# Splitting eleven weight units of the stick-breaking layer early, and keeping the two parts in DRAM

## The chip, the cores and the metric

The kernel runs on one core of a Trainium2 chip. The metric is the time of one execution on the device in microseconds. The engines of the core are TensorE (PE, with its weight loads PEld), VectorE (DVE), ScalarE (ACT), GpSimd (POOL) and SyncE (SP), which here only issues DMAs.

## The reference, cut to what matters

Two blocks follow each other on 512 tokens of width 1024, all in float32.

The first block is a hybrid layer: a norm, one wide projection `proj = h @ w_in`, a state-space branch with a convolution over four tokens, a sliding-window attention branch, gates, an output projection, and then 64 routed experts.

The second block puts 16 learned tokens in front (528 rows) and runs a stick-breaking attention layer, a wide layer with a squared ReLU, a differential attention layer and another wide layer. What the change touches is the projection of the stick-breaking layer:

```python
hn = rmsnorm(h, a_norm_g[i])
qkv = (hn @ a_w_qkv[i]).reshape(B, T, 3, SB_HEADS, SB_HEAD_DIM)
q, k, v = (qkv[:, :, x].transpose(0, 2, 1, 3) for x in range(3))   # cut
o = stick_breaking_attention(q, k, v)   # weights sigmoid(z) * product of (1 - sigmoid(z)) over later keys
h = h + merge_heads(o) @ a_w_o[i]
```

The matrix `a_w_qkv` is an input: nothing has to be computed before its split can be made.

## The kernel before

**Split matmuls.** A float32 product is computed as three matmuls of a rounded type: each operand is split into a high part (a copy that rounds, on ScalarE) and a low part (operand minus high part, on VectorE), and the products high x high, high x low and low x high are summed (`mm3`, `mm3s`). Every weight matrix is laid out on the host in units of 256 output columns: 128 partitions by 2048 floats, 1 MB. A unit is loaded by SyncE into one of three buffers `raw` (`load`, line 139) and split into one of two buffers `wh` and one of two `wl`.

**The first block's projections.** `block1_body` first normalizes and transposes x. Then `dense_x` (units 0 to 3 of the state-space columns) makes two tiles per unit: 24 matmuls of 512 columns, then the convolution on ScalarE and VectorE, a tanh one tile later, and a store of the result to DRAM. After it come six units of the query, key, value and time-step columns, each with four token tiles of 24 matmuls. Their results stay on the chip in twelve `dq` tiles. The window attention (`swa`) begins after that, with further units of `dense_x` and `dense_z` woven between its steps.

Working tiles of the first block come from one pool of 44 slots of 128 partitions by 516 floats (`S`). Results of matmuls lie in eight banks.

**The stick-breaking layer.** It has 12 units: for each of four groups of heads one unit of q, one of k and one of v. The list is made in `a_units` (line 779), followed by eight pieces of the output weights. `ahead` and `start_unit` (line 170) load a unit, take its two split buffers, and prepare four split pieces of 512 columns; `tick` issues one piece while the unit before it is being multiplied, and `take` issues what is left, hands the unit out and starts the next. The first unit is loaded and split at the end of the experts. `layer_a` runs the units of group 0 at once, and weaves those of groups 1 to 3 between the steps of the heads (`sb_steps`): scores on TensorE, softplus on VectorE and ScalarE, a scan on VectorE (L2029), a subtraction on GpSimd (L2030), an exponential on ScalarE (L2031), then transpositions and the product with v. In this part TensorE's instructions keep the order in which they are written.

**What else sets the order.** Apart from the instructions that are pinned, a list scheduler decides the order on every engine ahead of time, SyncE's queue included: instructions stand in the order in which they would be ready in its own model, earlier program positions first. On the chip every engine then works through its list in order, so a DMA that waits for a semaphore holds up the DMAs behind it.

Of the kernel before, what the change touches and what calls it, by code (L numbers as in the profile page):

```python
# [9 lines left out]
F32 = mybir.dt.float32  # L10
F32R = mybir.dt.float32r
# [55 lines left out]
class K:  # L67
# [47 lines left out]
    def pin(self, ins):  # L115
        return self.tc.keep_in_program_order(ins)
# [53 lines left out]
    def start_unit(self):  # L170
        self.unit = None
        if self.units:
            src, w, K = self.units.pop(0)
            pin, self.pin_unit = self.pin if self.pin_unit else lambda x: x, False
            raw = self.load(src, w)
            h = self.st.tile([128, 2112], F32R, tag="wh", bufs=self.NSPL, name="wh")
            l = self.st.tile([128, 2112], F32R, tag="wl", bufs=self.NSPL, name="wl")

            def pieces():
                for i in range(0, w, w // 4):  # L180
                    x = slice(i, i + w // 4)
                    pin(self.nc.scalar.activation(h[:, x], raw[:, x], AF.Copy))
                    pin(self.nc.vector.tensor_tensor(l[:, x], raw[:, x], h[:, x].bitcast(F32), op=ALU.subtract))  # L183
                    yield
            self.unit = [t[:, :w].rearrange("p (k c) -> p k c", k=K) for t in (h, l)], pieces()
# [113 lines left out]
    def rest(self, fills):  # L299
        for f in fills:  # L300
            for _ in f:
                pass


    def block1(self):
        pool = self.tc.tile_pool
        with pool(name="cp1", bufs=1) as self.cp, pool(name="sm1", bufs=1) as self.sm, pool(name="act1", bufs=1) as self.act:
            self.block1_body()

    def block1_body(self):  # L310
# [12 lines left out]
        conv = self.small(I["conv"], [128, 24, 5], "conv")  # L323
# [15 lines left out]
        with self.in_order("scalar", "vector"):  # L339
            W0 = self.split_steps(raw0, 2048)  # L340
# [6 lines left out]
            W0 = [next(W0), self.load_split(I["w_xbc"][1], 2048)]  # L347
# [12 lines left out]
                            ("gate_d", [2, 512, 1024]), ("oT_d", [8, 128, 512])):  # L360
            setattr(self, name, self.dr.tile(shape, F32, name=name))
        self.wide = 2
        self.rest([self.dense_x(conv, 0, 4, W0)])


        cs = self.sincos(posi)
# [6 lines left out]
        for u in range(6):  # L373
            w = 264 if u < 4 else 256
            src = I["w_dq264"][u] if u < 4 else I["w_dq256"][u - 4]
            wh, wl = self.load_split(src, 8 * w)
            for t in range(4):
                p = self.PD()
                ts = slice(t * 128, (t + 1) * 128)
                self.mm3(p[:, :w], lambda k: hh[k][:, ts], lambda k: hl[k][:, ts], lambda k: wh[:, k], lambda k: wl[:, k])  # L380
                self.evac(dq[t][u // 2][:, (u % 2) * 256:(u % 2 + 1) * 256], p[:, :256])
                if u < 4:
                    nc.vector.tensor_copy(dtr[:, t, 8 * u:8 * u + 8], p[:, 256:264])
            if u == 3:
                self.dt_prep(dtr, dtb, alg)

        self.wide = 1
        fills = [self.dense_x(conv, 4, 12), self.dense_z(0, 4)]
# [35 lines left out]
        for _ in self.ssd_out(3, self.last_norm, acc):  # L424
            n, t = step // 4, step % 4
# [353 lines left out]
    def a_units(self):  # L779

        W = self.I["a_w_o"]
        return [(self.I["a_w_qkv"][i + hg], 2048, 8) for hg in range(4) for i in (0, 4, 8)] + [(W[u][:, :1280], 1280, 5) for u in range(4)] \
            + [(W[u][:, 1280:], 768, 3) for u in range(4)]

    def last_rows(self):
# [1861 lines left out]
```

## Time and profile before

| | us |
|---|---|
| median of 3 runs | 2669.95 (2668.76 to 2676.37) |
| the profiled execution | 2671.22 |
| its span, first to last instruction | 2669.4 |
| TensorE busy in the span | 2534.5 |
| VectorE, ScalarE, GpSimd busy | 1517.1, 1108.8, 538.0 |
| mean granted clock of TensorE | 0.982 |

Busy time is the union of an engine's instructions. In a row of the windows view, each engine has its busy time in that stretch and, in brackets, the number of its instructions; the clock is the granted share of full speed, and the DMA share is the mean over 16 engines. An instruction's row ends with the idle time before it and what ended it. The first block's projections lie from about 22 to 140 us, the experts from about 740 to 1260 us, the stick-breaking layer from about 1290 to 1630 us.

### The profile page before, as it was taken

The page shows a single profiled execution, that of the slowest core. Times are in us where ns is not written, and L with a number is a line of the kernel's source. Part 1 is how long each engine was busy: PE and PEld are TensorE (multiplying, and loading weights), DVE is VectorE, ACT ScalarE, POOL GpSimd, SP SyncE. Part 2 cuts the span into 40 slices and gives each one's busy share as a digit, 9 for nine tenths or more (in the row PEclk, how much of TensorE's full clock was granted, in tenths as well). Part 3 has the DMA queues.
Part 4 walks back from the last instruction along what each step waited for, and adds up shares of the span by engine and source line. Part 5 has one row for each costly group of instructions (what it writes and reads, how often), then busy time and mean ns, then how long its engine had stood idle before and what let it go on. Part 6 is the DMA issues. An engine that isn't in the chain of part 4 may idle for free. (4 is left out here: it accounts for less than half of the span.)

```text
span 2669.4 us, 43757 instructions
## 1 busy us (share of the span) xinstructions
PE 2534.5 (95%) x17386; PEld 2114.4 (79%) x17386; DVE 1517.1 (57%) x3166; ACT 1108.8 (42%) x2261; POOL 538.0 (20%) x537
## 2 busy tenths in 40 slices
PE   7998999999979998997999999999999899999999
PEld 5987769879955555553888889999999777788887
DVE  6488666686652222224588886334467878634433
ACT  5356644433311111112498764223245766523321
POOL 0043532221121100111154420001102445100000
PEclk9999999999989999999899999999999999999999
DMA  5223365445399999998311323222231011322221
GB/s 191 94 103 131 115 202 179 165 146 187 111 388 392 419 419 419 411 384 344 113 57 37 114 76 118 95 94 82 95 116 64 32 57 49 118 81 94 95 95 63
DMA packets 111360, 436.86 MB, mean 164 GB/s; under 512 B 16441, under 2 KB 37353, under 8 KB 68912
## 3 DMA queue, kind: packets, MB, share of 16 engines
q1 hardware_dynamic: 105488, 429.33, 43.3%
q0 software_dynamic: 5520, 4.63, 0.7%
q8 instruction: 138, 2.26, 0.3%
q14 instruction: 70, 0.57, 0.1%
q10 hardware_dynamic: 144, 0.07, 0.0%
HBM read 400.65 MB, written 43.79 MB: 166 GB/s over the span
## 5 line engine op out<-in xcount | busy, mean ns | idle before, releaser
L210 DVE TENSOR_TENSOR wl<-raw,wh 128x1024 fp32r<-128x1024 f32 (+2 forms) x228 | 280.4, 1260 | 212.5 <-ACT wh L209 208.5
L232 PE MATMUL pd<-hh,wh 128*128 128x512 f32 (+2 forms) x1152 | 393.9, 343 | 4.4 <-DVE zth L1333 2.9
L232 PE MATMUL pd<-hl,wh 128*128 128x512 f32 (+2 forms) x1152 | 392.9, 342 | 2.7 <-DVE hl L213 2.7
L232 PE MATMUL pd<-hh,wl 128*128 128x512 f32 (+2 forms) x1152 | 393.7, 343 | 1.0 <-DVE wl L245 1.0
L209 ACT ACTIVATE wh<-raw 128x1024 fp32r<-128x1024 f32 (+2 forms) x228 | 222.7, 1022 | 412.9 <-PE pd L232 312.7
L232 PE MATMUL pd<-wh,hh 128*128 128x256 f32 (+2 forms) x936 | 266.8, 285 | 4.5 <-DVE vt L2380 1.8
L232 PE MATMUL pd<-wl,hh 128*128 128x256 f32 (+2 forms) x936 | 264.1, 282 | 2.2 <-DVE wl L213 2.2
L232 PE MATMUL pd<-wh,hl 128*128 128x256 f32 (+2 forms) x936 | 264.4, 283 | 0.0
L232 PEld LDWEIGHTS pd<-hh,wh 128*128 128x128 f32 x1152 | 218.3, 190 | 30.1 <-DVE zth L1333 3.1
L232 PEld LDWEIGHTS pd<-hl,wh 128*128 128x128 f32 x1152 | 218.6, 190 | 29.0 <-DVE hl L213 2.9
L232 PEld LDWEIGHTS pd<-hh,wl 128*128 128x128 f32 x1152 | 218.3, 190 | 27.3 <-DVE wl L245 1.9
L1027 PE MATMUL pd<-mraw,xg 128*48 128x256 f32 x2048 | 237.6, 384 | 2.2 <-DMA mraw<-in_w_moe 2.2
L1027 PEld LDWEIGHTS pd<-mraw,xg 128*48 128x48 f32 x2048 | 128.2, 124 | 92.5 <-issue 10.8
L232 PEld LDWEIGHTS pd<-wh,hh 128*128 128x128 f32 (+1 forms) x936 | 170.5, 182 | 10.3 <-issue 2.7
L232 PEld LDWEIGHTS pd<-wl,hh 128*128 128x128 f32 (+1 forms) x936 | 170.4, 182 | 4.4 <-DVE wl L213 2.7
L232 PEld LDWEIGHTS pd<-wh,hl 128*128 128x128 f32 (+1 forms) x936 | 170.1, 182 | 1.9 <-issue 0.2
L1035 DVE TENSOR_TENSOR sg<-lo,pd 48x256 f32<-48x256 f32 x64 | 27.1, 423 | 223.3 <-ACT lo L1034 223.3
L987 POOL DMA_INDIRECT y_d<-ys,idx x64 | 60.5, 945 | 435.0 <-DVE ys L1061 411.1
L232 PE MATMUL pd<-vh,wl 128*128 128x272 f32 (+1 forms) x512 | 145.2, 285 | 0.0
L232 PE MATMUL pd<-vl,wh 128*128 128x272 f32 (+1 forms) x512 | 145.2, 285 | 0.0
L232 PE MATMUL pd<-vh,wh 128*128 128x272 f32 (+1 forms) x512 | 143.5, 284 | 0.0
L232 PE MATMUL pd<-wh,xh 128*128 128x256 f32 (+1 forms) x384 | 124.0, 325 | 0.5 <-DVE acc L1399 0.3
(593 smaller groups left out, 6150.7 us busy)
## 6 DMA issues: line engine op xcount, KB each, us to landing
mraw<-in_w_moe SPq DMA_DIRECT2D x192, 1024.0 KB
raw<-in_mlp_w_in SPq DMA_DIRECT2D x32, 1024.0 KB
raw<-in_mlp_w_out SPq DMA_DIRECT2D x32, 1024.0 KB
raw<-in_w_xbc SPq DMA_DIRECT2D x12, 1024.0 KB
raw<-in_a_w_qkv SPq DMA_DIRECT2D x12, 1024.0 KB
raw<-in_w_z SPq DMA_DIRECT2D x8, 1024.0 KB
raw<-in_w_gate_in SPq DMA_DIRECT2D x8, 1024.0 KB
bc<-acT_d SPq DMA_DIRECT2D x32, 256.0 KB
```

Source lines behind the costliest of these rows:

```text
L209: nc.scalar.activation(h, src, AF.Copy)
L210: nc.vector.tensor_tensor(l, src, h.bitcast(F32), op=ALU.subtract)
L232: self.nc.tensor.matmul(*a, **kw)
L987: x = self.nc.gpsimd.indirect_dma_start(out=self.y_d[:, :], out_offset=bass.IndirectOffsetOnAxis(ap=rows, axis=0), in_=y[0:64 + self.CAP], ...
L1027: self.pin(self.nc.tensor.matmul(p[64 * i:64 * i + self.CAP, 0:256], lhsT=x[:, k], rhs=w[i][:, k], start=k == 0, stop=k == 7))
L1035: self.nc.vector.tensor_tensor(sg[0:CAP], lo, p[64:64 + CAP, 0:256], op=ALU.mult)
```

## The change

Units 1 to 11 of `a_w_qkv` are no longer loaded and split in the layer. A new generator `presplit` walks through them in steps of 512 columns: a load of 256 KB into a working tile, a copy on ScalarE, a subtraction on VectorE, and two stores of 256 KB into a new DRAM tensor `aw_d`, one for the high parts and one for the low parts. There are 44 steps. Two are issued after each of the last six of the first eight convolution tiles; then one or two after each token tile of the six units that follow; what is left, if anything, before the window attention. In the layer `start_unit` loads the two parts of such a unit straight into `wh` and `wl`, on SyncE, when the unit is started, and its `pieces` yield nothing. Unit 0 and the output weights are split as before.

```diff
-            raw = self.load(src, w)
+            raw = None if isinstance(src, list) else self.load(src, w)
             h = self.st.tile([128, 2112], F32R, tag="wh", bufs=self.NSPL, name="wh")
             l = self.st.tile([128, 2112], F32R, tag="wl", bufs=self.NSPL, name="wl")
 
+            if raw is None:
+                for t, x in zip((h, l), src):
+                    self.nc.sync.dma_start(t[:, :w].bitcast(F32), x)
+
             def pieces():
-                for i in range(0, w, w // 4):
+                for i in range(0, w if raw is not None else 0, w // 4):
...
+    def presplit(self):
+
+        self.aw_d = self.dr.tile([2, 12, 128, 2048], F32, name="aw_d")
+        for u in range(1, 12):
+            for c in range(0, 2048, 512):
+                c = slice(c, c + 512)
+                raw, h, l = self.S(name="awr")[:, :512], self.S(F32R, name="awh")[:, :512], self.S(F32R, name="awl")[:, :512]
+                self.nc.sync.dma_start(raw, self.I["a_w_qkv"][u, :, c])
+                self.split_to(h, l, raw)
+                for x, y in enumerate((h, l)):
+                    self.nc.sync.dma_start(self.aw_d[x, u, :, c], y.bitcast(F32))
+                yield 1
...
-        self.rest([self.dense_x(conv, 0, 4, W0)])
+        pre = self.presplit()
+        for i, _ in enumerate(self.dense_x(conv, 0, 4, W0)):
+            for _ in range(2 if i > 1 else 0):
+                next(pre)
...
                 if u < 4:
                     nc.vector.tensor_copy(dtr[:, t, 8 * u:8 * u + 8], p[:, 256:264])
+                for _ in range(1 + (t % 2)):
+                    next(pre, None)
             if u == 3:
                 self.dt_prep(dtr, dtb, alg)
+        self.rest([pre])
...
-        return [(self.I["a_w_qkv"][i + hg], 2048, 8) for hg in range(4) for i in (0, 4, 8)] + [(W[u][:, :1280], 1280, 5) for u in range(4)] \
+        return [((self.I["a_w_qkv"][i + hg] if hg + i == 0 else [self.aw_d[x, i + hg] for x in range(2)]), 2048, 8) for hg in range(4) for i in (0, 4, 8)] + [(W[u][:, :1280], 1280, 5) for u in range(4)] \
```

## Rows read from the trace of the kernel before

**Rows 1.** The page, parts 1 and 2: span, and TensorE's busy time

```profile
span 2669.4 us, 43757 instructions
...
PE 2534.5 (95%) x17386; PEld 2114.4 (79%) x17386; DVE 1517.1 (57%) x3166; ACT 1108.8 (42%) x2261; POOL 538.0 (20%) x537
```

**Rows 2.** Windows view: stretch, length, busy time (count) per engine, clock, DMA, GB/s

```profile
20.00:140.00 120.00, 117.24 (x787) 106.38 (x785) 67.91 (x141) 56.45 (x83) 3.41 (x3) 1.00 0.32 112
140.00:170.00 30.00, 30.00 (x133) 24.16 (x132) 22.64 (x36) 17.53 (x26) 11.54 (x14) 1.00 0.38 132
170.00:200.00 30.00, 30.00 (x131) 24.02 (x130) 27.98 (x51) 16.07 (x25) 16.32 (x24) 1.00 0.27 95
200.00:220.00 20.00, 13.98 (x60) 10.77 (x58) 19.83 (x33) 13.49 (x20) 9.56 (x12) 0.91 0.50 172
1340.00:1520.00 180.00, 162.66 (x1230) 152.19 (x1229) 149.77 (x282) 148.76 (x309) 85.98 (x73) 0.94 0.22 70
...
1290.00:1340.00 50.00, 46.77 (x362) 44.33 (x361) 29.32 (x55) 25.23 (x49) 11.30 (x11) 0.93 0.20 68
```

**Rows 3.** Waits of TensorE, 1340 to 1520 us: total, times, longest

```profile
PE pm L245 <- ACT zs L2031: 8.8, 4, 3.4
PE pd L245 <- DVE kT L1885: 3.4, 2, 1.9
...
PE pd L245 <- DVE wl L183: 2.3, 3, 0.8
PE pd L245 <- ACT wh L182: 0.5, 1, 0.5
```

**Rows 4.** Timeline in the layer: start, duration, engine, line, operation, idle before

```profile
1375.79 2.19 ACT L182 ACTIVATE wh<-raw 128x512 fp32r<-128x512 f32 x4
...
1400.52 2.21 ACT L182 ACTIVATE wh<-raw 128x512 fp32r<-128x512 f32 x4
...
1402.90 1.89 DVE L183 TENSOR_TENSOR wl<-raw,wh 128x512 fp32r<-128x512 f32 x3
...
1403.98 0.63 ACT L2031 ACTIVATE zs<-zs 128x528 f32<-128x528 f32 x1
...
1404.66 1.33 PE L245 MATMUL pm<-consts,zs 128*128 128x128 f32 x5 [3.41 <-ACT zs L2031]
```

**Rows 5.** Windows view in steps of 2 us around that wait

```profile
1400.00:1402.00 2.00, 0.55 (x3) 0.31 (x3) 2.00 (x5) 2.00 (x5) 1.30 (x1) 1.00 0.30 70
...
1404.00:1406.00 2.00, 1.34 (x6) 1.26 (x7) 2.00 (x5) 2.00 (x5) 0.15 (x1) 0.50 0.45 61
```

**Rows 6.** Groups by form, 1290 to 1520 us: count, busy us, mean ns

```profile
L183 DVE TENSOR_TENSOR wl<-raw,wh 128x512 fp32r<-128x512 f32 x44 | 34.5, 830 | 1.4 <-ACT wh L182 1.3
...
L183 DVE TENSOR_TENSOR wl<-raw,wh 128x320 fp32r<-128x320 f32 x4 | 1.7, 478 | 0.0
...
L182 ACT ACTIVATE wh<-raw 128x512 fp32r<-128x512 f32 x44 | 24.2, 621 | 9.1 <-PE pd L232 9.1
L182 ACT ACTIVATE wh<-raw 128x320 fp32r<-128x320 f32 x4 | 1.5, 454 | 0.0
```

**Rows 7.** Windows view of the split's two lines alone, VectorE's and ScalarE's

```profile
1340.00:1520.00 180.00, 25.23 (x32) 0.94 0.22 70
...
1340.00:1520.00 180.00, 16.82 (x32) 0.94 0.22 70
```

**Rows 8.** The split's subtraction over the whole run: shortest, median, longest ns

```profile
L183 DVE TENSOR_TENSOR wl<-raw,wh x80: 342/678/1814, 1255.4 to 1600.0; 128x512 fp32r<-128x512 f32 x48, 128x320 fp32r<-128x320 f32 x16, 128x192 fp32r<-128x192 f32 x16
```

**Rows 9.** Windows view of two stretches in which DMA is crowded

```profile
1490.00:1500.00 10.00, 9.53 (x79) 9.30 (x77) 9.55 (x16) 7.78 (x16) 3.60 (x4) 1.00 1.01 366
...
425.00:430.00 5.00, 4.37 (x40) 3.98 (x39) 5.00 (x6) 3.58 (x6) 3.17 (x2) 1.00 0.99 341
```

**Rows 10.** Timeline of SyncE in the first block's projections

```profile
61.74 0.33 SPq L142 DMA_DIRECT2D raw<-in_w_dq  x1
...
72.95 0.33 SPq L142 DMA_DIRECT2D raw<-in_w_dq  x1
```

**Rows 11.** Waits of TensorE, 20 to 250 us

```profile
PE pm L1294 <- DVE cr L1481: 4.1, 1, 4.1
```

## The prediction

> **What bounds the kernel now.** I read the page first, then the windows view over the two stretches that the change touches, then the waits of TensorE, the timeline behind its longest wait, and last the rows of the split itself. The page says that TensorE is busy for 2534.5 of 2669.4 us, so only 135 us of the whole span are idle, and an edit can win time only where such idle time lies [rows 1]. The windows view shows where it does not lie: from 20 to 140 us, the first block's projections, TensorE is busy for 117.2 of 120 us at full clock, and from 140 to 200 us without a gap; VectorE and ScalarE are little more than half busy before 140 us [rows 2]. From 1340 to 1520 us, the heads of the stick-breaking layer, the picture is another: TensorE is busy for 162.7 of 180 us, VectorE for 149.8, ScalarE for 148.8, and the granted clock is 0.94. With levels of 2.4 and 1.2 GHz that mean says that some 0.12 x 180 = 21.6 us ran at the lower one.
>
> The waits there name ScalarE's exponential (zs L2031) for 8.8 us in 4 waits, then VectorE's kT for 3.4, and the split's own wl and wh for 2.8 us [rows 3]. The timeline behind one 3.41 us wait shows why: ScalarE starts four split pieces at 1400.52 and the exponential, for which TensorE stands, starts at 1403.98; VectorE has three of the subtractions from 1402.90 on [rows 4]. Behind that gap the clock is at its lower level: 1.00 from 1400 to 1402 us, 0.50 from 1404 to 1406 us [rows 5]. TensorE's order is written out there, so it stops whenever the chain score, softmax, exponential, transposition is late by more than the projections put in between can fill. So the limit of this stretch is that chain on two engines that are 83% busy, and the split is load that need not be on them.
>
> **What the change takes out of the layer.** Eleven units of four pieces leave: 44 VectorE subtractions, 34.5 us busy, and 44 ScalarE copies, 24.2 us [rows 6]. Sixteen pairs run from 1290 to 1340 us, where VectorE and ScalarE are little more than half busy and TensorE 46.8 of 50 us [rows 2]; I cost those at nothing, and if all that idle time were theirs they would be worth 3 us. The other 28 pairs, seven units, lie between 1340 and 1520 us. The split takes 25.2 us of VectorE and 16.8 us of ScalarE there, of which four smaller pieces of the output weights (1.7 and 1.5 us) stay [rows 6, 7]. So VectorE falls from 149.8 to 126.3 us and ScalarE from 148.8 to 133.5 us: 70% and 74% of the stretch instead of 83%. What can be won is the idle time, 180 - 162.7 = 17.3 us, and the work not done at the lower clock, 21.6 / 2 = 10.8 us, if every such dip follows a gap as the one shown does: 28 us in all. The least is nothing: of the waits only 2.8 us name the split itself, and the scans and the work on GpSimd in the chain stay. Seven bursts, each of which holds ScalarE for 2.2 us, set the chain back by 15 us if none of it is covered, which with the clock comes near the upper end. I take half of the 28 us, 14 us; both ends stay in the range.
>
> The split's VectorE pieces take 830 ns on average in this stretch, while their median over the run is 678 ns and the longest is 1814 ns [rows 6, 8], so they also suffer from something beside them. The Trainium skill (SBUF — State Buffer, section Who interferes with whom) says that a VectorE instruction with two inputs in SBUF and a GpSimd instruction that reads SBUF exclude each other for a whole instruction, and the split has two such inputs. By that rule the GpSimd steps of the chain would also get shorter, and the saving would lie nearer to 20 us than 14; the rows show only that the pieces are stretched, not what they do to GpSimd.
>
> **What it adds in the layer.** Instead of one load of 1 MB per unit there are two, straight into the buffers that TensorE reads. 11 MB more over some 230 us, where DMA is busy for 22% [rows 2], is nothing. But the buffers are two deep: a unit's load can start only when TensorE has finished with the unit before the last, and its wait stands in SyncE's queue ahead of whatever follows (stores of head outputs, later loads). Two megabytes at the 366 GB/s of the nearest crowded stretch [rows 9] take 5.7 us; two consecutive bursts lie 25 us apart [rows 4], so some 19 us of cover are left and I cost it at nothing. If that cover went, each unit would cost up to 6 us. The first such unit needs a buffer that the combination of the expert outputs reads last, and is wanted only after the 96 matmuls of unit 0, which come behind that combination.
>
> **What it adds in the first block.** 44 steps, 12 beside the convolution tiles and the rest beside the next projection. Each has a load of 256 KB, one copy, one subtraction, and two stores of 256 KB. On VectorE that is 44 x 0.68 = 30 us, on ScalarE 44 x 0.62 = 27 us (the same shape in [rows 6, 8]). From 20 to 140 us VectorE is idle for 52 and ScalarE for 64 us [rows 2], so both fit, and TensorE has eight banks of results to run ahead of late evacuations. On SyncE 132 issues of 0.33 us [rows 10] make 44 us, which fits too.
>
> DMA is tighter. The steps move 132 x 256 KB = 34.6 MB. The trace moves transfers of this size at 341 GB/s where the engines are 99% busy [rows 9]; that makes 101 us. The engines are 32% busy over the 120 us, so 82 us are free [rows 2]. Some 19 us of transfers, a fifth of the steps, are therefore left at 140 us. Eight or nine steps, 6 us of VectorE, then fall in the stretch from 140 to 220 us, where VectorE is busy for 70.5 of 80 us and where TensorE already stops 4.1 us for VectorE's cr [rows 2, 11]. What could hide it is the 7 us that VectorE has free until 170 us. I take 5 us of loss. The lower end is 0; the upper is that TensorE itself follows DMA, 19 us, and more where the queue's order is bad: I allow 30.
>
> The Trainium skill (DMA: Bandwidth & Descriptors, section Rules for kernel authors) asks for 1 MiB or more per transfer, and its section on the anatomy of one DMA gives, for DMAs issued by GpSimd, a fit of 2.0 us and the bytes at 436 GB/s; by it 256 KB take an estimated 2.6 us, 343 us for all if none overlapped. The row of 341 GB/s at transfers of this size speaks against the serial reading: there they overlap.
>
> **The sum.** The profiled execution took 2671.2 us: 2669.4 of span and 1.8 around it. 2671.2 - 14 + 5 = 2662.2. The median of the three timed runs is 2669.95, 1.3 us below that execution, so the forecast is 2661 us, faster by 0.34%. I treat 0.3%, 8 us, as what a measurement here can tell from nothing. Its own range, gain 8 to 20 us and loss 0 to 8, is 2648 to 2668.
>
> **Rivals.**
> 1. *The gain is not there* (26%). The chain of scans, GpSimd subtraction and exponential sets the pace, and the pieces only filled its gaps. For it: the waits on the split itself are 2.8 us of 17.3 idle, and the 3.4 us for kT name a projection's result, which no piece makes. Against: both engines are 83% busy, and the longest wait has pieces right before it [rows 3, 4]. Gain 4, loss 4: 2670 us.
> 2. *DMA holds the first block* (23%, slower). SyncE's queue is one order fixed ahead of time. If the stores of a step stand in it before a projection's weights and the loads land later than planned, the weights wait, and ScalarE and VectorE stand at a piece whose data is missing, ahead of the weight split. A projection unit takes 11.2 us between its loads [rows 10]; six steps beside it bring 4.7 MB, with its own weights 5.8 MB, 17 us at 341 GB/s. That is 6 us too much per unit, over six units 36 us, of which loads up to three units ahead and the idle DMA time at the start cover a sixth to a half. It decides once the transfers in front of a weight load exceed what three buffered units cover, some 25 us. Price 19 to 30 us: 2661 + 24 = 2685.
> 3. *The new loads stand in SyncE's queue at the wrong place in the layer* (4%, slower): a wait for TensorE's release ahead of the stores that free score buffers. Seven units at 3 us with the gain lost: 2690 us.
>
> The remaining 47% is the forecast. Faster by over 0.3%: 0.47; within 0.3%: 0.26; slower by over 0.3%: 0.27. For 8 times in 10 the range takes in rival 1 and most of rival 2: 2642 to 2689 us, the low end being most of the 28 us won at no cost.
>
> **What the profile after would show.** Right: in the layer VectorE's and ScalarE's busy time down by 24 and 15 us, waits for zs and wl gone or halved, the stretch shorter by some 14 us and its clock above 0.94; from 20 to 140 us DMA busy above 80% with TensorE still at 117 of 120 us; VectorE a few us busier from 140 to 220 us. Wrong: TensorE waiting for wh or wl of the projections between 60 and 170 us (rival 2), waits for zs of the same length in the layer (rival 1), or TensorE waiting for a DMA into wh or wl there (rival 3).

## The result, and the profile after

The changed kernel takes 2808.11 us (median of five runs, 2801.80 to 2812.21) where the kernel before takes 2673.17 us: a ratio of 1.0502, 95% interval 1.0490 to 1.0515. Forecast were 2661 us and a range of 2642 to 2689. It is 135 us slower, and the range missed it by 119 us.

The page of the changed kernel, to be set beside [rows 1]: TensorE executes the same number of matmuls, yet it is idle for 2800.0 - 2547.7 = 252 us instead of 135.

```profile
span 2800.0 us, 44077 instructions
...
PE 2547.7 (91%) x17386; PEld 2126.0 (76%) x17386; DVE 1514.7 (54%) x3166; ACT 1111.4 (40%) x2261; POOL 539.7 (19%) x537
```

Three instructions that both kernels have serve as milestones: the load of `iota`, issued when the experts begin; the first `lastq`, ahead of the stick-breaking layer; and the last sum of squares (`pm<-sq,ones`), behind its heads. Each row gives an instruction's count, its min/median/max in ns, and the starts of the first and the last one. First the kernel before, then the changed one:

```profile
L659 SPq DMA_DIRECT2D iota<-in_consts x1: 333/333/333, 738.1 to 738.1; - x1
...
L126 DVE TENSOR_SCALAR lastq<-iota,slot,gw x8: 406/408/414, 1228.3 to 1231.9; 128x256 f32<-128x256 f32 x8
...
L1705 PE MATMUL pm<-sq,ones x8: 377/386/392, 1305.8 to 1629.2; 128*128 128x256 f32 x4, 128*128 128x272 f32 x4
```

```profile
L682 SPq DMA_DIRECT2D iota<-in_consts x1: 333/333/333, 884.4 to 884.4; - x1
...
L126 DVE TENSOR_SCALAR lastq<-iota,slot,gw x8: 403/409/412, 1374.7 to 1378.3; 128x256 f32<-128x256 f32 x8
...
L1728 PE MATMUL pm<-sq,ones x8: 377/386/393, 1450.5 to 1762.1; 128*128 128x256 f32 x4, 128*128 128x272 f32 x4
```

Up to the experts 884.4 - 738.1 = 146.3 us are lost. The stick-breaking layer, from `lastq` to the last sum of squares, is 387.4 us long instead of 400.9: 13.5 us won. The difference of the two is 132.8 us. The two traces differ by 2800.0 - 2669.4 = 130.6 us; the 2 us between these numbers lie behind the layer. So the layer gains about as much as was forecast, and the whole miss lies in the first block.

The windows view of the changed kernel, with the columns of [rows 2]. The last row is the stretch that answers to 1340 to 1520 us of before, 144.7 us later:

```profile
20.00:140.00 120.00, 92.83 (x526) 81.77 (x525) 62.59 (x115) 48.33 (x72) 0.20 (x2) 0.89 0.63 196
140.00:170.00 30.00, 7.81 (x65) 7.59 (x63) 8.42 (x12) 6.94 (x9) 0.00 (x0) 0.71 0.74 218
170.00:200.00 30.00, 8.56 (x48) 8.38 (x48) 6.50 (x19) 4.32 (x8) 0.00 (x0) 0.61 0.55 160
...
40.00:290.00 250.00, 142.28 (x820) 128.59 (x820) 87.53 (x174) 75.70 (x120) 8.02 (x7) 0.77 0.63 194
1484.70:1664.70 180.00, 169.26 (x1344) 158.99 (x1343) 142.91 (x273) 147.09 (x308) 92.46 (x83) 0.98 0.38 130
```

The kernel before does the same 820 matmuls from 40 us on in about half that time:

```profile
40.00:166.00 126.00, 125.23 (x821) 113.91 (x820) 72.91 (x155) 56.09 (x86) 13.47 (x16) 1.00 0.33 115
```

From 40 to 290 us TensorE stands still for 107.7 us, and its 820 matmuls take 142.3 us instead of 125.2, at a mean granted clock of 0.77 instead of 1.00. That is 124 of the 146 us. The other 22 us are lost behind it: from there to the `iota` load the changed kernel takes 884.4 - 290 = 594.4 us, the kernel before 738.1 - 166 = 572.1 us. And from 140 to 200 us no engine is near its limit: VectorE and ScalarE work for 28% of the time or less, and DMA is 74% and 55% busy. Where every resource has room, the time must go into waiting, so the next view is the waits. First TensorE from 20 to 420 us, then ScalarE and SyncE's queue up to 350 us (total, times, longest, in us):

```profile
PE pd L236 <- DVE dtr L403: 50.2, 3, 39.7
PE pd L236 <- ACT cc L1496: 32.4, 6, 13.8
PE pd L236 <- DVE acT L1150: 18.9, 1, 18.9
...
ACT awh L213 <- DMA awr<-in_a_w_qkv: 164.4, 42, 6.6
...
SPq L318 <- ACT awh L213: 142.5, 38, 5.5
```

TensorE waits for banks that copies of its results have to empty (`dtr` on VectorE, `cc` on ScalarE). ScalarE waits for the load of a step, 42 times for 44 steps; and SyncE's queue waits for ScalarE's copy of a step, 38 times. These two wait for each other in turn, as the timeline of two steps shows (start, duration, engine, line; the idle time before it in brackets):

```profile
154.54 0.63 ACT L213 ACTIVATE awh<-awr 128x512 fp32r<-128x512 f32 x1 [5.41 <-DMA awr<-in_a_w_qkv]
...
155.19 0.32 SPq L318 DMA_DIRECT2D aw_d<-awh  x1
155.20 0.69 DVE L214 TENSOR_TENSOR awl<-awr,awh 128x512 fp32r<-128x512 f32 x1 [5.35 <-ACT awh L213]
155.56 0.42 SPq L315 DMA_DIRECT2D awr<-in_a_w_qkv  x1
156.08 0.40 SPq L318 DMA_DIRECT2D aw_d<-awl  x1
...
159.72 0.63 ACT L213 ACTIVATE awh<-awr 128x512 fp32r<-128x512 f32 x1 [2.66 <-DMA awr<-in_a_w_qkv]
160.38 0.32 SPq L318 DMA_DIRECT2D aw_d<-awh  x1
160.38 0.69 DVE L214 TENSOR_TENSOR awl<-awr,awh 128x512 fp32r<-128x512 f32 x1 [1.88 <-ACT awh L213]
160.75 0.42 SPq L315 DMA_DIRECT2D awr<-in_a_w_qkv  x1
```

Read it in a circle. The copy ends at 155.17; only then can SyncE issue the store of the high part (155.19), which stands in its queue ahead of the next load (155.56); that load lands just before the next copy (159.72); and so on. One load of a step is on its way at a time. The rows of the two tiles give the length of a round: the load lands 4.1 us (median) after its issue, the copy takes 0.63, the store's and the load's issue 0.3 to 0.4 each, and 43 rounds lie between the first copy and the last, (281.5 - 48.7) / 43 = 5.41 us each:

```profile
L315 SPq DMA_DIRECT2D awr<-in_a_w_qkv x44: 336/424/832, 41.9 to 278.1; - x44
...
DMA to landing us min/median/max: 3.1/4.1/6.3
...
L213 ACT ACTIVATE awh<-awr x44: 615/630/636, 48.7 to 281.5; 128x512 fp32r<-128x512 f32 x44
```

What that does to TensorE is seen in VectorE's list while TensorE stands for 39.7 us (VectorE from 148 to 188 us, and TensorE's next matmul; the subtractions at 155.20 and 160.38 are shown above):

```profile
149.16 0.69 DVE L214 TENSOR_TENSOR awl<-awr,awh 128x512 fp32r<-128x512 f32 x1 [1.92 <-ACT awh L213]
...
165.44 0.69 DVE L214 TENSOR_TENSOR awl<-awr,awh 128x512 fp32r<-128x512 f32 x1 [4.36 <-ACT awh L213]
171.73 0.69 DVE L214 TENSOR_TENSOR awl<-awr,awh 128x512 fp32r<-128x512 f32 x1 [5.60 <-ACT awh L213]
176.12 0.69 DVE L214 TENSOR_TENSOR awl<-awr,awh 128x512 fp32r<-128x512 f32 x1 [3.70 <-ACT awh L213]
181.99 0.69 DVE L214 TENSOR_TENSOR awl<-awr,awh 128x512 fp32r<-128x512 f32 x1 [5.18 <-ACT awh L213]
...
186.62 0.69 DVE L214 TENSOR_TENSOR awl<-awr,awh 128x512 fp32r<-128x512 f32 x1 [2.91 <-ACT awh L213]
187.23 0.23 DVE L403 COPY dtr<-pd 128x8 f32<-128x8 f32 x2
...
187.54 0.55 PE L236 MATMUL pd<-wh,hh 128*128 128x256 f32 x1 [39.73 <-DVE dtr L403]
```

Results of projections lie in the banks, and the copies that would empty them stand in VectorE's list behind subtractions, each of which waits for its own round. Eight of them come before the `dtr` copies at 187.23, behind which TensorE starts again.

### The profile page after: what moved, and what is told of

It reads as the page before. It is cut to its first block, busy times and chain, and to the rows that moved or that the text cites. A ratio compares the mean times of both kernels' runs of the same rounds, so it can differ in the third digit from the quotient of the medians.

```text
span 2800.0 us, 44077 instructions
## 1 busy us (share of the span) xinstructions
PE 2547.7 (91%) x17386; PEld 2126.0 (76%) x17386; DVE 1514.7 (54%) x3166; ACT 1111.4 (40%) x2261; POOL 539.7 (19%) x537
## 5 line engine op out<-in xcount | busy, mean ns | idle before, releaser
L214 DVE TENSOR_TENSOR wl<-raw,wh 128x1024 fp32r<-128x1024 f32 (+2 forms) x228 | 279.0, 1254 | 204.0 <-ACT wh L213 199.4
L236 PE MATMUL pd<-wh,hh 128*128 128x256 f32 (+2 forms) x936 | 273.1, 292 | 87.3 <-DVE dtr L403 50.2
L1050 PEld LDWEIGHTS pd<-mraw,xg 128*48 128x48 f32 x2048 | 129.2, 124 | 91.0 <-issue 11.5
L1010 POOL DMA_INDIRECT y_d<-ys,idx x64 | 60.3, 943 | 435.3 <-DVE ys L1084 411.3
```

What stands on the lines that cost most here:

```text
L214: nc.vector.tensor_tensor(l, src, h.bitcast(F32), op=ALU.subtract)
L236: self.nc.tensor.matmul(*a, **kw)
L1010: x = self.nc.gpsimd.indirect_dma_start(out=self.y_d[:, :], out_offset=bass.IndirectOffsetOnAxis(ap=rows, axis=0), in_=y[0:64 + self.CAP], ...
L1050: self.pin(self.nc.tensor.matmul(p[64 * i:64 * i + self.CAP, 0:256], lhsT=x[:, k], rhs=w[i][:, k], start=k == 0, stop=k == 7))
```

## The experiments

The theories, with the letters that the expectations use. A: the steps go round one at a time, so the loss is a count of rounds. B: it is the bytes, 34.6 MB on busy DMA engines. C: it is the pieces' own time on ScalarE and VectorE in front of other work. For the runs in which several loads are on their way, D is the limit of DMA and E the engines' work. In the runs below, the loss of the first block is the shift of the `iota` load, and the layer is measured between the same two milestones as above, both in one trace per kernel. A run given with a ratio was timed four times or more, the others once; fourteen timings of the kernel before spread from 2663.05 to 2675.05 us, so differences of a few us between single runs say nothing. The edits are cut to the lines that matter.

**1. The first half alone.** The 44 steps stay; the layer loads and splits its units as before.

```diff
-        return [((... if hg + i == 0 else [self.aw_d[x, i + hg] for x in range(2)]), 2048, 8) ...
+        return [((... if hg + i == 0 else self.I["a_w_qkv"][i + hg]), 2048, 8) ...
```

> The early split and its stores stay in the first block, but the layer loads and splits all its units as before (the stored parts are not read). All theories that put the loss into the first block: about 2673 + 146 = 2819 us, 13 us over the changed kernel, the layer as long as before. If the loads into wh and wl in the layer were part of the loss: below 2808 us.

Measured: 2813.29 us; first block +148.1, layer -0.6. So the steps with their stores make the whole loss, and the loads in the layer have no part in it.

**2. The second half alone.** The layer reads ready parts eleven times, but only unit 1 is split early and its parts are read in place of all eleven: the other units' weights are left out.

```diff
-        for u in range(1, 12):
+        for u in range(1, 2):
...
-                next(pre)
+                next(pre, None)
...
-        ... else [self.aw_d[x, i + hg] for x in range(2)]), 2048, 8) ...
+        ... else [self.aw_d[x, 1] for x in range(2)]), 2048, 8) ...
```

> Only unit 1 is split early (4 steps instead of 44), and the layer loads unit 1's two parts for all eleven units, so its results are those of other weights; loads, bytes and matmuls in the layer are the changed kernel's. If the layer's gain is real and independent of the first block: first block within 3 us of before, layer 12 to 15 us shorter, 2657 to 2663 us in all. Rival: the layer only looked shorter because the kernel came to it in another state: within 4 us of before.

Measured: 2658.36 us, ratio 0.9954 (0.9937 to 0.9970); first block +0.9, layer -14.2. The window over the heads of this kernel is that of the changed kernel, clock included:

```profile
1341.00:1521.00 180.00, 169.23 (x1343) 158.95 (x1342) 141.19 (x272) 146.70 (x307) 92.49 (x82) 0.98 0.37 128
```

The two halves add up: 148.1 - 14.2 = 133.9, and the whole change shows 132.8. Four steps at the beginning cost next to nothing (+0.9); their last copy starts at 65.4 us.

**3. Loads written eight steps ahead.** The same 44 steps, loads and stores, in the same places, but eight loads are written before the first step and one more before each:

```diff
+        for _ in range(8):
+            load()
+        for n, (u, c) in enumerate(steps):
...
+                load()
+                raw, h, l = raws[n], self.S(F32R, name="awh")[:, :512], self.S(F32R, name="awl")[:, :512]
```

> The loads of the early split are written eight steps ahead of the copies, subtractions and stores; same bytes, same operations. Theory A (one step at a time: a load stands in SyncE's queue behind the store of the step before, so each of the 44 steps costs a full round trip of about 5.5 us, and ScalarE and VectorE stand waiting for it in front of TensorE's evacuations): most of the 146 us goes, first block 5 to 30 us longer than before, 2665 to 2695 us in all. Theory B (34.6 MB more do not fit beside the projections): DMA is as busy as in the changed kernel and the time stays within 20 us of 2808. Theory C (the pieces themselves fill VectorE and ScalarE ahead of the evacuations): also within 20 us of 2808.

Measured: 2673.74 us, ratio 1.0004 (0.9995 to 1.0014); first block +22.3, layer -16.6. Of 146 us, 124 are gone with no byte and no instruction less. That is theory A, and it rules out B and C as the cause of those 124. The rounds shrink to (157.9 - 48.2) / 43 = 2.55 us, and now DMA is full over 130 us:

```profile
40.00:170.00 130.00, 126.42 (x819) 115.26 (x818) 91.64 (x178) 73.90 (x120) 11.06 (x12) 0.99 1.02 356
```

The copies of its steps (min/median/max in ns, first and last start):

```profile
L213 ACT ACTIVATE awh<-awr x44: 612/620/635, 48.2 to 157.9; 128x512 fp32r<-128x512 f32 x44
```

Up to 170 us TensorE is less than 3 us behind: it is busy for 126.4 of these 130 us, and for 129.2 in the kernel before. So most of the 22 us that are left are lost later, when DMA has room again. By what chain was not followed up; run 6 tells what they hang on.

**4. The stores issued by GpSimd.** A narrower form of A: only the store in SyncE's queue holds the next load back.

```diff
-                    self.nc.sync.dma_start(self.aw_d[x, u, :, c], y.bitcast(F32))
+                    self.nc.gpsimd.dma_start(self.aw_d[x, u, :, c], y.bitcast(F32))
```

> The 88 stores are issued by GpSimd, the 44 loads stay on SyncE and are written where the change has them; same bytes. Theory A in its narrow form (the store in SyncE's queue is what holds the next load): loads run ahead on the chip and most of the 146 us goes, 2670 to 2710 us. Theory A in its wider form (the next load also waits for a slot that the step before frees, because slots are handed out in the written order): little goes, 2770 us or more. Theory B: within 20 us of 2808.

Measured: 2733.82 us; first block +74.0, layer -14.4, a round 3.76 us. It fell between what the two forms expected, so it decides for neither. Half of the loss goes with the stores out of SyncE's queue. For the other half the trace names a suspect: from 40 to 210 us SyncE's queue waits 87.8 us, in 11 waits, at the load of a projection's weights until the split before it frees a buffer (`wl` L214), and loads of steps stand behind it; six of them then go out together from 108.1 us on. No run tests that.

**5. Buffers of their own.** One line: the step's load goes into three buffers of its own instead of a slot of the pool of 44.

```diff
-                raw, h, l = self.S(name="awr")[:, :512], self.S(F32R, name="awh")[:, :512], ...
+                raw, h, l = self.act.tile([128, 512], F32, tag="awr", bufs=3, name="awr"), self.S(F32R, name="awh")[:, :512], ...
```

> One edit to the change: the raw tiles of the early split come from three buffers of their own instead of the shared pool of 44 slots; everything is written in the change's order. Theory A with its cause in the pool (slots of one pool are handed out in the written order, so the load of the next step can't be placed ahead of the copy of this one): the scheduler moves loads ahead by itself, the chip does not stand for them, and most of the 146 us goes: 2670 to 2710 us, nearer to the upper end than with eight steps ahead because only three loads run ahead. If the pool has nothing to do with it: 2790 us or more.

Measured: 2691.49 us; first block +45.1, layer -20.7. The written order of the steps is that of the changed kernel; only where the load lands is other. The first load now starts at 14.7 us instead of 41.9, and a round takes 3.38 us:

```profile
L315 SPq DMA_DIRECT2D awr<-in_a_w_qkv x44: 328/484/851, 14.7 to 184.0; - x44
...
L213 ACT ACTIVATE awh<-awr x44: 613/630/635, 44.8 to 190.1; 128x512 fp32r<-128x512 f32 x44
```

So it is the shared pool that keeps the load of a step behind the step before it. With buffers of their own SyncE's queue has three loads in a row (from 14.67, 111.44 and 125.59 us), ahead of the stores of the steps before them. From the code I read it so: slots of one pool are handed out in the order in which the tiles are written, a step takes one for its load and then two for its parts, and the scheduler therefore can't place the next load ahead of those. That reading is argued, the effect is shown. Why the layer gains 20.7 us here, more than in any other run, stays open.

**6. Eight ahead, and no stores.** What the 22 us of run 3 are: the two stores are left out, and the layer splits its units as before.

```diff
                 for x, y in enumerate((h, l)):
-                    self.nc.sync.dma_start(self.aw_d[x, u, :, c], y.bitcast(F32))
+                    pass
```

> As with the loads eight steps ahead, but the parts are not stored (23 MB less), and the layer splits its units as before, so nothing of the early work is used. What is left of the loss in the first block with eight steps ahead is 22 us. Theory D (it is DMA, busy at 1.04 from 60 to 160 us there): with a third of the bytes the first block costs 0 to 6 us, 2672 to 2680 us in all. Theory E (it is the 30 us of VectorE and 27 us of ScalarE): it still costs 15 us or more, 2688 us or more.

Measured: 2675.48 us; first block +4.9, layer -3.6. The pieces of all 44 steps are still executed, so their time on ScalarE and VectorE costs at most 4.9 us; the other 17 us of run 3 go with the stores. So it is not E. The run takes away the stores' bytes and their places in SyncE's queue at once; that it is the bytes, D, is argued from DMA's share, 0.59 here against 1.02 in run 3, and from runs 7 and 8, which keep stores in that queue, have DMA 85% and 90% busy over the same 130 us, and lose 3.6 and 4.5 us:

```profile
40.00:170.00 130.00, 129.23 (x840) 117.16 (x839) 106.38 (x204) 83.72 (x136) 17.66 (x18) 1.00 0.59 202
```

The copies of its steps (min/median/max in ns, first and last start):

```profile
L213 ACT ACTIVATE awh<-awr x44: 613/621/640, 48.7 to 135.5; 128x512 fp32r<-128x512 f32 x44
```

**7. Seven units, eight loads ahead.** Only the seven units whose split falls among the heads are moved (28 steps, one per tile), so DMA has less to do; the layer loads and splits the other four as before.

```diff
-        steps = [(u, slice(c, c + 512)) for u in range(1, 12) for c in range(0, 2048, 512)]
+        steps = [(u, slice(c, c + 512)) for u in (9, 2, 6, 10, 3, 7, 11) for c in range(0, 2048, 512)]
...
-            for _ in range(2 if i > 1 else 0):
-                next(pre)
+            for _ in range(1 if i > 1 else 0):
+                next(pre, None)
...
-                for _ in range(1 + (t % 2)):
+                for _ in range(1):
...
```

> Loads eight steps ahead, but only the seven units that before were split between 1340 and 1520 us are split early (28 steps, 22 MB instead of 35), one step per tile. By theory D the first block then has room for the transfers and costs 2 to 8 us, while the layer keeps most of its gain (9 to 13 us): 2662 to 2668 us, faster than both kernels. If the four units before them carry the gain, or if VectorE and ScalarE set the loss: 2672 us or more.

Measured: 2656.82 us, ratio 0.9946 (0.9933 to 0.9959): faster than both kernels, by half a per cent against the kernel before. First block +3.6, layer -13.0. The four units left out were worth little: 13.0 and 13.5 are not told apart by one trace each. And DMA is no longer full in the first block:

```profile
20.00:140.00 120.00, 117.13 (x783) 106.32 (x782) 84.08 (x164) 69.45 (x108) 2.75 (x4) 1.00 0.87 294
```

The copies of its steps (min/median/max in ns, first and last start):

```profile
L213 ACT ACTIVATE awh<-awr x28: 614/622/638, 49.1 to 135.7; 128x512 fp32r<-128x512 f32 x28
```

**8. All eleven units, spread out.** Four loads ahead, one step per tile, and what is left over beside the state-space branch.

```diff
...
-        self.rest([pre])
...
-        self.weave(self.ssd(dskT, sgT, acc, ya, fills), fills, None)
+        self.weave(beside(self.ssd(dskT, sgT, acc, ya, fills)), fills, None)   # beside: next(pre, None) after every step
+        self.rest([pre])
```

> All eleven units, loads four steps ahead, one step per tile in the projections (30 steps) and the last 14 steps one at a time between the steps of the state-space branch, from some 350 us on. By theory D the first block costs less than the 22 us of eight steps ahead, 5 to 12 us, and the layer gains 12 to 17: 2662 to 2672 us. If the late steps hold that branch up (slots and order again): 2680 us or more.

Measured: 2660.82 us, ratio 0.9963 (0.9950 to 0.9975); first block +4.5, layer -14.6. Its interval and that of run 7 overlap, so the two are not told apart. It shows that also the whole change pays once its rounds overlap and its bytes are spread.

**9. Two loads ahead.** The edit of run 3 with 2 in place of 8.

```diff
-        for _ in range(8):
+        for _ in range(2):
```

> As with eight steps ahead, but two. Theory A in numbers: a step takes about 5.4 us because one load is on its way at a time; with two written ahead two or three are, so the steps come every 2 to 3 us, nearer to what DMA can carry (768 KB at 360 GB/s, 2.2 us): first block 25 to 60 us longer than before, between eight steps ahead (22) and none (146), near to three buffers of their own (45); 2685 to 2720 us in all. If only a long lead helps: 2760 us or more.

Measured: 2693.65 us; first block +46.0, layer -16.4. A round takes 3.03 us: between one load at a time (5.41) and many (2.55).

```profile
L213 ACT ACTIVATE awh<-awr x44: 612/632/634, 48.2 to 178.5; 128x512 fp32r<-128x512 f32 x44
```

**10. Seven units, none ahead.** Run 7 with the steps as the change writes them. It asks whether fewer steps alone would have done.

```diff
-        for u in range(1, 12):
+        for u in (9, 2, 6, 10, 3, 7, 11):
...
```

> The seven units of the fastest version, one step per tile, but written as the change has them, no load ahead. Theory A: 28 steps of 5.4 us make 151 us for tiles that take 110 us, so it loses most of what the change loses per step: first block 50 to 95 us longer, 2710 to 2755 us in all. If the amount of data alone made the difference: within 5 us of 2657.

Measured: 2727.34 us; first block +71.0, layer -12.9. A round takes 5.77 us, with DMA 69% busy from 40 to 170 us. A smaller dose of the same thing loses less, but still 71 us.

```profile
40.00:170.00 130.00, 103.25 (x690) 96.38 (x688) 62.71 (x133) 49.72 (x77) 1.68 (x1) 0.88 0.69 211
```

The copies of its steps (min/median/max in ns, first and last start):

```profile
L213 ACT ACTIVATE awh<-awr x28: 616/632/635, 49.5 to 205.2; 128x512 fp32r<-128x512 f32 x28
```

Put together, the loss of the first block follows the time by which the last step ends too late. In runs 7 and 6, which lose 4 to 5 us, the last copy of a step starts at 135.7 and 135.5 us; so I count from 135.6:

| kernel | one round | last copy starts | later than 135.6 | first block loses |
|---|---|---|---|---|
| changed kernel | 5.41 | 281.5 | 146 | 146.3 |
| 1, first half alone | 5.39 | 278.9 | 143 | 148.1 |
| 4, stores on GpSimd | 3.76 | 210.5 | 75 | 74.0 |
| 10, seven units, none ahead | 5.77 | 205.2 | 70 | 71.0 |
| 5, own buffers | 3.38 | 190.1 | 55 | 45.1 |
| 9, two ahead | 3.03 | 178.5 | 43 | 46.0 |
| 3, eight ahead | 2.55 | 157.9 | 22 | 22.3 |
| 7, seven units, eight ahead | 3.21 | 135.7 | 0 | 3.6 |
| 6, eight ahead, no stores | 2.02 | 135.5 | 0 | 4.9 |

Run 5 lies 10 us off this rule, the others 5 or less. Run 8 is not in the table: its last 14 steps stand beside later work, the last copy starts at 411.0 us, and it loses 4.5 us. So a late step costs only what is held up behind it.

## Why the prediction was wrong

**The layer was right.** 14 us were forecast, 13.5 were won, 14.2 in run 2. The mechanism holds too: between the two milestones TensorE's idle time falls from 40.9 to 34.3 us, and its busy time from 360.0 to 353.1 us with the clock at 0.96 instead of 0.94. That the size fits so well is partly luck, since 14 was simply half of what could be won. VectorE and ScalarE did not fall by 24 and 15 us per window as said (142.9 and 147.1 us against 149.8 and 148.8), because the same 180 us now hold 1344 matmuls instead of 1230: the stretch is denser, which is the gain itself. Between the milestones they fall by 27.4 and 22.4 us. In the window the clock rose from 0.94 to 0.98 and TensorE's idle time fell from 17.3 to 10.7 us. The waits of TensorE in the layer (1484 to 1665 us) show the split's own waits gone, as forecast, and `kT` down from 3.4 to 1.1 us; the exponential, which was to be gone or halved, still has 6.9 us where it had 8.8 [rows 3]:

```profile
PE pm L249 <- ACT zs L2054: 6.9, 3, 2.8
PE pd L249 <- DVE v L217: 2.2, 1, 2.2
PE pd L249 <- DVE kT L1908: 1.1, 1, 1.1
```

So rival 1 is false. The sixteen pairs that I costed at nothing were worth little: run 7 leaves them in place and has 13.0 us. A microsecond or two can't be read from these numbers: in the seven kernels that read all eleven units ready the layer gains 13.5 to 20.7 us, and in runs 1 and 6, whose layer is that of before, 0.6 and 3.6. Rival 3 is false too: the loads into `wh` and `wl` are on their way for 5.1 and 6.8 us, by the median, and no wait of TensorE names one. The row for `wh`:

```profile
L181 SPq DMA_DIRECT2D wh<-aw_d x11: 319/332/544, 1416.1 to 1626.6; - x11
...
DMA to landing us min/median/max: 4.7/5.1/6.9
```

**The rule on the shared port.** By the Trainium skill (SBUF — State Buffer, section Who interferes with whom) a VectorE instruction with two inputs in SBUF contends with a GpSimd instruction that reads SBUF. I concluded that the subtraction on GpSimd would become shorter when the split left, and the saving come nearer to 20 us. Neither came: the commonest form takes 1055 ns before and 1054 after. First the kernel before, then the changed one, GpSimd's subtraction among the heads, both from 1340 to 1680 us, where the last four of the changed kernel are missing:

```profile
L2030 POOL TENSOR_TENSOR zs<-zs,zd 128x384 f32<-128x384 f32 x32 | 33.8, 1055 | 56.3 <-DVE zd L2029 35.0 <-PE pd L245 4.8 <-ACT zs L257 3.7
```

```profile
L2053 POOL TENSOR_TENSOR zs<-zs,zd 128x384 f32<-128x384 f32 x28 | 29.5, 1054 | 33.4 <-DVE zd L2052 30.0 <-ACT o16w L2173 3.1
```

Over the whole layer the 52 subtractions of all forms take 60.9 us before and 60.3 after. So GpSimd's own times hardly changed; whether the two engines held each other up before is not shown.

**The step that failed: the first block at 5 us.** It was worked out from capacities: so much busy time of VectorE, ScalarE and DMA beside so much that is free, and "on SyncE 132 issues of 0.33 us make 44 us, which fits too". As sums of busy time they hold: run 6 shows that the engines' work costs at most 5 us. Of the bytes I took 5 us of loss and kept 19 as an upper end; with overlapping rounds they cost 17 to 22 us (runs 3 and 6), so the upper end was the better figure, though TensorE did not lose it while DMA was full, as I had thought, but later. All this is small beside the miss. What the sums take for granted is that loads of different steps overlap. They did not: a load waited for the store of the step before, that store for the copy, and the copy for its load. The missing term is 44 rounds of 5.41 us, 238 us in a stretch of about 95 us between the first step and the last projections of the kernel before; the difference is 143 us, and 146 were measured. The sign that was to show a right forecast, TensorE at 117 of 120 us with DMA above 80% from 20 to 140 us, came out as 92.8 us and 63%.

I had the pieces of it. In the changed kernel a waiting store holds up the load behind it in SyncE's queue (142.5 us of waits for `awh`), and rival 2 said that this order could matter and named the place: ScalarE and VectorE at a piece whose data is missing, ahead of what TensorE waits for. But I priced that rival by its bytes, 19 to 30 us, and not by the time from issue to landing of one load and the number of loads, and I looked for the wait at `wh` and `wl` while most of it came by way of the banks. Rival 2 is therefore true in the place that it names, wrong in the way by which most of the wait reaches TensorE, and low by a factor of five to eight in its price. Two sums beside it are off as well, without bearing on the miss: a gain of 8 to 20 us with a loss of 0 to 8 makes 2650 to 2670 us, not 2648 to 2668, and rival 3 with the loss of 5 us in the first block makes 2696 us, not 2690.

The trace of before could not show this wait: its weight loads go into three buffers of their own, and from 40 to 166 us neither ScalarE nor VectorE waits for one. The sentence on the Trainium skill (DMA: Bandwidth & Descriptors, the section on the anatomy of one DMA) held the reading that came nearest: it asked what the sum would be if nothing overlapped, 343 us for 132 transfers at an estimated 2.6 us each (a load here landed after 4.1 us, by the median). I dismissed it with the row of 341 GB/s [rows 9], which shows that transfers of this size can overlap; whether these would is a question on the order of the queue. As it turned out, the stores of a step do overlap with the next load, and the loads of the steps do not overlap with one another.

## What to carry to other kernels

Before pricing a load, compute and store step by its bytes, write down the order of its DMAs in the queue that issues them: where the store of step n stands ahead of the load of step n+1, the steps take their count times the full round from issue to landing to store, here 44 times 5.4 us, and what of it the stretch does not cover anyway (here some 95 us) is the price. Write the loads several steps ahead of their use, or give them buffers of their own, and see that the engines which empty TensorE's banks hold no instruction that waits for them. Then move only as much as pays: here seven units of eleven bring nearly the whole gain.

## What the runs showed of the hardware that was not expected

A load of 256 KB that SyncE issues lands 3.1 to 6.3 us after its issue (median 4.1) while DMA is only 63% busy. With loads on their way side by side the median is 6.2 us in run 5, with DMA 93% busy from 40 to 170 us. Loads and stores, some three quarters of their bytes those of the steps, in rows of 2 KB, reach 356 GB/s at a busy share of 1.02 in run 3, between the 341 GB/s of [rows 9] that I had used and the 366 beside it.
